# Pacing the background work of a decoder block: dearer choices, an idle background beside the query products, a gate table in four parts, and choices placed next to their gathers

## The chip, the cores and the metric

The kernel runs on one core of a Trainium2 chip. The metric is the device time of one execution in microseconds. Most executions of this kernel agree within 0.3%.

## The reference

One decoder block on 1024 tokens of width 1024, in float32. The second half of it is what the change is about:

```python
def peer_ffn(h, w_query, sub_keys, expert_u, expert_v):
    q = jnp.einsum('bsd,dk->bsk', h, w_query).reshape(B, S, 8, 2, 128)
    sc = jnp.einsum('bshpc,hpnc->bshpn', q, sub_keys)
    s1, i1 = lax.top_k(sc[..., 0, :], 16)
    s2, i2 = lax.top_k(sc[..., 1, :], 16)
    cand_s = (s1[..., :, None] + s2[..., None, :]).reshape(B, S, 8, 256)
    cand_i = (i1[..., :, None] * 128 + i2[..., None, :]).reshape(B, S, 8, 256)
    top_s, sel = lax.top_k(cand_s, 16)
    idx = jnp.take_along_axis(cand_i, sel, axis=-1)
    gates = jax.nn.softmax(top_s, axis=-1)
    ...
    u = expert_u[ec]
    a = jax.nn.gelu(jnp.einsum('cd,chkd->chk', xc, u), approximate=False) * wc
    return jnp.einsum('chk,chkd->cd', a, expert_v[ec])
```

The first half of the block is a normalisation, one wide input projection, a causal pooling mixer and a forgetting attention of 16 heads, an output projection and a residual addition. Each token then chooses 128 of 16384 experts (8 heads, 16 each), and an expert is one row of `expert_u` and one of `expert_v`.

## The kernel before

**Phases.** The tokens go through the first half in three phases of 512, 256 and 256 tokens, numbered 0, 1 and 2 (`phase`). A phase does attention with its input projections (`w_in`), then the output projection (`w_out`), then the query products (`w_query`, 16 chunks), each chunk followed on DVE by the top 16 of the scores. Matrix products in float32 are done as three products of high and low halves (`mm3`), and the halves of a weight are made by ScalarE (high) and DVE or POOL (low). Phases 0, 1 and 2 hold token tiles 0 to 3, 4 and 5, 6 and 7, of 128 tokens each.

**Two ways of computing the experts.** Tiles 1 to 5 (640 tokens) are computed densely: all 16384 experts are multiplied through, in 16 groups. A group is eight calls of `up` (a weight of 512 KB, 48 products, Gelu, times the gate table, split into halves `ah`, `al`) and eight of `down` (a weight, 48 products, added into `accT`). The gate table of a group, `Gg`, 2560 KB, is read back from DRAM, where `gates` wrote it. `finish_dense` transposes, normalises and stores. Tiles 0, 6 and 7 are computed by `experts`: 128 gathers of rows of `peer_u` by an indirect DMA issued on POOL (L900), each with a dot product on DVE (L915), then 128 of `peer_v`, each accumulated on DVE (L925), then the end of the tile (L929 to L939). The gathers are kept in program order on POOL; five row buffers are in turn.

**Background work.** `choose(tt)` turns the scores of a tile into 128 expert numbers and gates, nearly all on DVE (L858 is its most frequent line, 32 instructions per choice). `gates(gb, tt)` turns a chosen dense tile into its part of the gate table with DVE, POOL, TensorE (L983, 32 units) and ScalarE, and writes it to DRAM. `choose`, `gates` and `experts` are generators: each `yield` gives the cost at which the piece of work before the next one is booked. The work in front (`proj`, the attention units, `up`, `down`) calls `tick(us)` with a planner's time of what it has just issued; `tick` adds that time times `bg["rate"]` to a credit, and background pieces are issued while the credit is positive:

```python
        bg["credit"] += us * bg["rate"]
        while bg["todo"] and bg["credit"] > 0:
            cost = next(bg["todo"][0], None)
            ...
                bg["credit"] -= cost
```

`drain` issues all that is left without asking for credit. `RATES` holds the rates: the first for phase 1, the second for the attention of phase 2, the fourth for its output projection and queries, the third for the dense stage. The list in phase 1 is choice 0, choice 1, gates 1, choice 2, gates 2, choice 3, gates 3; phase 2 adds choice 4, gates 4, choice 5, and behind its attention gates 5. What is left is drained before the dense stage. There the list is choices 6 and 7, then the gathers of tiles 0, 6 and 7.

What the generators fix is the order of the program. A scheduler then sets the order on each engine: an instruction that is ready may go ahead of earlier ones that are not, except those that are kept in program order.

Of the kernel before, what the change touches and what calls it, by code (L numbers as in the profile page):

```python
# [37 lines left out]
XJ = 5  # L38
HP = 500
WX = (0, 0, 0)  # L40
RATES = (0.75, 0.6, 0.68, 0.7)
WL = ((0, 1), (0, 1), (0, 1))
C_U, C_Q, C_K, C_V, C_F, C_GA, C_GB = 0, 4, 12, 20, 28, 29, 37

# [2 lines left out]
def block_kernel(ctx: ExitStack, tc: tile.TileContext, I, out, dbg=None):  # L47
# [433 lines left out]
    def phase(c, nxt):  # L481
# [294 lines left out]

        tv = [sel.tile([128, PH, 2, 16], F, name="mv", tag="mv", bufs=4) for _ in range(NQ)]
        tx = [sel.tile([128, PH, 2, 16], U32, name="mxi", tag="mxi", bufs=4) for _ in range(NQ)]
        for ch in range(16):
            h, half = ch // 2, ch % 2  # L780
            z = proj(c, ("w_query", ch), h2h, h2l) if ch else z0
            if p == 2 and ch % 2:
                for x in range(2):
                    tc.keep_in_program_order(mv(W["h2"][x][:, ch // 2], h2dT[x][:, ch // 2]))
            q2 = c.tile("full", 3)
            nc.scalar.activation(q2, z, AF.Copy)
            ky = big.tile([128, 128], F, name="ky", tag="ky", bufs=2)
            nc.sync.dma_start(ky, I["keys"][ch])
            ps = pt_tile()[:, :n]
            for i in range(NQ):  # L790
                nc.tensor.matmul(ps[:, i * 128:(i + 1) * 128], q2[:, i * 128:(i + 1) * 128], ky,
                                 start=True, stop=True)
            sc = big.tile([128, n], F, name="sc", tag="sc", bufs=1)
            nc.scalar.activation(sc, ps, AF.Copy)
            for i in range(NQ):
                s_ = sc[:, i * 128:(i + 1) * 128]
                m_, x_ = tv[i][:, h, half], tx[i][:, h, half]
                tmp = sel.tile([128, 128], F, name="tmp", tag="tmp", bufs=2)
                nc.vector.max(m_[:, 0:8], s_)
                nc.vector.max_index(x_[:, 0:8], m_[:, 0:8], s_)  # L800
                nc.vector.match_replace(tmp, m_[:, 0:8], s_, -3e38)
                nc.vector.max(m_[:, 8:16], tmp)
                nc.vector.max_index(x_[:, 8:16], m_[:, 8:16], tmp)
        store_parts()
        big.release()
        return nc_, [choose(qb0 + i, tv[i], tx[i]) for i in range(NQ)]

    def choose(tt, mv_, mx_):
# [8 lines left out]
        for o, r0, r1, w in ((0, 0, 2, 16), (32, 2, 4, 8), (48, 4, 16, 4)):  # L817
# [1 line left out]
            full = [128, PH, r1 - r0, w]  # L819
            nc.vector.tensor_tensor(dst, a1[:, :, r0:r1, None].to_broadcast(full),  # L820
                                    b1[:, :, None, 0:w].to_broadcast(full), op=OP.add)
        yield 3.0
        ts = sel.tile([128, PH, 16], F, name="ts", tag="ts", bufs=1)
        ti = sel.tile([128, PH, 16], U32, name="ti", tag="ti", bufs=1)
        for h in range(PH):
            tmp = sel.tile([128, 128], F, name="tmp", tag="tmp", bufs=2)[:, :96]
            nc.vector.max(ts[:, h, 0:8], cand[:, h])
            nc.vector.max_index(ti[:, h, 0:8], ts[:, h, 0:8], cand[:, h])
            nc.vector.match_replace(tmp, ts[:, h, 0:8], cand[:, h], -3e38)
            nc.vector.max(ts[:, h, 8:16], tmp)  # L830
            nc.vector.max_index(ti[:, h, 8:16], ts[:, h, 8:16], tmp)
            if h % 2:
                yield 1.8
        tif = ti.rearrange("p h k -> p (h k)")
        ra, rb, w0, w1, pf = (pk[:, i * 128:i * 128 + 128] for i in range(5))
        u0 = sel.tile([128, 128], U32, name="u0", tag="u0", bufs=1)
# [16 lines left out]
        for half, r, dst in ((0, ra, w0), (1, rb, w1)):  # L853
            r4 = r.rearrange("p (h k) -> p h k", k=16)
            for part, to in ((0, dst), (1, pf)):
                for x in range(8):
                    v = mxf[:, :, half, part * 8 + x:part * 8 + x + 1].to_broadcast([128, PH, 16])
                    nc.vector.scalar_tensor_tensor(oh[:, :, :, x], r4, float(part * 8 + x), v,  # L858
                                                   op0=OP.is_equal, op1=OP.mult)
                    if x % 4 == 3:  # L860
                        yield 0.8
                nc.vector.tensor_reduce(to, oh.rearrange("p h k x -> p (h k) x"), axis=AX.X, op=OP.add)
                yield 1.1
            nc.vector.tensor_add(dst, dst, pf)
        gt = sel.tile([128, PH, 16], F, name="gate", tag="gated" if dense else f"gate{tt}", bufs=1)
        nc.vector.tensor_tensor(gt, ts, ts[:, :, 0:1].to_broadcast([128, PH, 16]), op=OP.subtract)
# [133 lines left out]
    def dense_experts():  # L1000
        h2h, h2l = W["h2"]
        wcount[1] = (0, 1)
        dd = tpool("dd", "right")
        W["x"], W["m"], W["i"] = dd, 1, 2
        X["p"] = dd
        acc = dd.tile([128, 8, ND], F, name="accT")
        A = {}

        def up(e):
            if e % 8 == 0:  # L1010
                A["G"] = dd.tile([128, NC16, 8, 16], F, name="Gg", tag="Gg", bufs=1)
                nc.sync.dma_start(A["G"], Gd[e // 8].rearrange("p c (i t) -> p c i t", i=8))
            wh, wl = load_w(I["ut"][e])
            G = A["G"][:, :, e % 8, :]
            A[e] = []
            for h in range(2):
                z = d_tile("z")[:, :NH]
                T = slice(h * NH, h * NH + NH)
                for k in range(8):
                    mm3(z, wh[:, k], wl[:, k], h2h[:, k, T], h2l[:, k, T], k == 0, k == 7)  # L1020
                ah = dd.tile([128, NH], R, name="ah", tag="ah", bufs=16)
                al = dd.tile([128, NH], R, name="al", tag="al", bufs=16)

                nc.scalar.activation(z, z, AF.Gelu)
                z3 = z.rearrange("p (c t) -> p c t", t=16)
                nc.vector.tensor_tensor(z3, z3, G[:, h * NC16 // 2:(h + 1) * NC16 // 2], op=OP.mult)
                split(ah, al, z, nc.vector)
                A[e].append((ah, al))
                tick(12 * ND * 0.00043)

        def down(gr, c):
            wh, wl = load_w(I["vt"][gr * 8 + c], nc.gpsimd)
            for h in range(2):
                o = d_tile("oT")[:, :NH]
                T = slice(h * NH, h * NH + NH)
                for i in range(8):
                    ah, al = A[gr * 8 + i][h]
                    mm3(o, wh[:, i], wl[:, i], ah, al, i == 0, i == 7)
                if gr == 0:
                    nc.vector.tensor_copy(acc[:, c, T], o)  # L1040
                else:
                    nc.vector.tensor_tensor(acc[:, c, T], acc[:, c, T], o, op=OP.add)
                if gr == 15:
                    nc.vector.scalar_tensor_tensor(acc[:, c, T], acc[:, c, T], gt2[:, c:c + 1], A["x1"][:, c, T],
                                                   op0=OP.mult, op1=OP.add)
            tick(24 * ND * 0.00043)

        def finish_dense(i, rows, fg):
            ps = [f() for f in ((pt_tile, pt_tile), (z_tile, z_tile), (s_tile, s_tile))[i % 3]]
            ss = cst.tile([128, 4], F, name="ss", tag="ssd", bufs=2)  # L1050
            yt = rows[:, i * D:i * D + D]
            hs = (slice(0, 512), slice(512, 1024))
            for hf, (pt, H) in enumerate(zip(ps, hs)):
                for c in range(4):
                    nc.tensor.transpose(pt[:, c * 128:(c + 1) * 128],
                                        acc[:, hf * 4 + c, i * 128:(i + 1) * 128], ident)
                nc.scalar.activation(yt[:, H], pt, AF.Square, accum_out=ss[:, hf:hf + 1])
            rs = rstd(ss)
            for pt, H in zip(ps, hs):
                nc.vector.scalar_tensor_tensor(yt[:, H], pt, rs, fg[:, H], op0=OP.mult, op1=OP.mult)  # L1060
            nc.sync.dma_start(out[(DT0 + i) * 128:(DT0 + i + 1) * 128, :], yt)

        for gr in range(16):
            for i in range(8):
                up(gr * 8 + i)
            if gr == 15:

                A["x1"] = W["hx"].tile([128, 8, ND], F, name="h2x0", tag="h2x0")
                fg = W["hx"].tile([128, ND // 128, D], F, name="h2x1", tag="h2x1")
                nc.sync.dma_start(A["x1"], x1dT)  # L1070
                nc.sync.dma_start(fg[:, 0], I["final_g"].partition_broadcast(128))
                rows = A["G"].rearrange("p a b c -> p (a b c)")
            for i in range(8):
                down(gr, i)
        for i in range(DT1 - DT0):
            finish_dense(i, rows, fg[:, 0])
        W["m"], X["p"] = 0, None
        drain()
        dd.release()
# [40 lines left out]
    bank["free"] = False  # L1120
    psx.release()
    X["ps"] = tc.alloc_tile_pool(name="psg", bufs=1, space=PS, reuse_waits="tile")
    bg["todo"] = ch + late + [experts(tt) for tt in range(DT1, 8)]
    bg["rate"] = RATES[2]
    dense_experts()
    X["ps"].release()
# [57 lines left out]
```

## Time and profile before

| | |
|---|---|
| median of three runs | 3362.7 us (3359.74 to 3367.93) |
| profiled execution, its own time | 3367.48 us |
| its span, first to last instruction | 3365.7 us |
| TensorE products, busy | 3132.3 us (93%), mean granted clock 0.968 |
| DVE, ScalarE, POOL busy | 2427.5, 1267.7, 1754.1 us |
| transfers | 1004.60 MB, mean 298 GB/s |

Busy shares are averages over stages with different limits: the dense stage, from about 1492 us on, and the phases before it are to be read one by one, by windows. TensorE's busy time is modelled from pipelined products; where it is full, the count of products in a window says more.

### The profile page before, as it was taken

How to read it: one execution, taken by the hardware profiler on the slowest of the kernel's cores; microseconds unless marked ns; L12 is line 12 of the kernel's file. 1: busy time of each engine (PE TensorE's matmuls, PEld its weight loads, DVE VectorE, ACT ScalarE, POOL GpSimd, SP SyncE). 2: the span in 40 equal slices, each digit the busy share in tenths (PEclk: the TensorE clock that was granted, in tenths of full speed). 3: DMA queues.
4: the chain of work that ended last, by engine and by line, in shares of the span. 5: the costliest groups of instructions: out<-in, count | busy, mean ns of one | idle time of the engine just before them, and what ended most of it. 6: DMA issues, size and time to landing. Idle time of an engine off the chain costs nothing. (4 is left out here: it accounts for less than half of the span.)

```text
span 3365.7 us, 56878 instructions
## 1 busy us (share of the span) xinstructions
PE 3132.3 (93%) x20912; PEld 2992.4 (89%) x20912; DVE 2427.5 (72%) x5520; ACT 1267.7 (38%) x2405; POOL 1754.1 (52%) x1328
## 2 busy tenths in 40 slices
PE   6999889888799899888999999999999999999995
PEld 4778778778788798888999999999999999999994
DVE  5764556997958876768766777677677767777677
ACT  5555542346545565522222322232223222322231
POOL 1233233013324132414777787678777767777774
PEclk9999999899999999999999999999999999999997
DMA  8987787777789788783899899899998999989997
GB/s 330 332 299 261 271 297 270 240 231 235 226 304 313 226 268 269 259 311 139 306 333 332 320 328 337 318 348 332 339 329 321 322 330 344 346 319 337 329 337 252
DMA packets 373078, 1004.60 MB, mean 298 GB/s; under 512 B 34128, under 2 KB 146368, under 8 KB 370624
## 3 DMA queue, kind: packets, MB, share of 16 engines
q1 hardware_dynamic: 262208, 598.26, 51.7%
q0 software_dynamic: 110592, 402.70, 32.7%
q8 instruction: 166, 2.72, 0.3%
q14 instruction: 112, 0.92, 0.1%
HBM read 851.25 MB, written 149.58 MB: 297 GB/s over the span
## 5 line engine op out<-in xcount | busy, mean ns | idle before, releaser
L233 POOL TENSOR_TENSOR wl<-wr,wh 128x1024 fp32r<-128x1024 f32 x320 | 776.1, 2426 | 647.7 <-ACT wh L232 604.4
L232 ACT ACTIVATE wh<-wr 128x1024 fp32r<-128x1024 f32 x325 | 344.2, 1059 | 927.5 <-PE oT L280 536.1
L279 PE MATMUL oT<-ah,wh 128*128 128x320 f32 x2048 | 632.3, 310 | 10.0 <-ACT ah L232 10.0
L279 PE MATMUL z<-h2x,wh 128*128 128x320 f32 x2048 | 633.8, 310 | 3.3 <-ACT wh L232 1.7
L281 PE MATMUL z<-h2x,wl 128*128 128x320 f32 x2048 | 633.5, 310 | 1.4 <-POOL wl L233 1.3
L280 PE MATMUL oT<-al,wh 128*128 128x320 f32 x2048 | 633.0, 310 | 1.2 <-DVE al L233 1.1
L280 PE MATMUL z<-h2x,wh 128*128 128x320 f32 x2048 | 633.3, 309 | 0.0
L281 PE MATMUL oT<-ah,wl 128*128 128x320 f32 x2048 | 632.7, 310 | 0.0
L925 DVE SCALAR_TENSOR_TENSOR acc<-g,dots,acc 128x1024 f32<-128x1024 f32 x381 | 489.2, 1284 | 124.9 <-DMA g<-peer_v,idx 122.3
L915 DVE SCALAR_TENSOR_TENSOR g<-g,h 128x1024 f32<-128x1024 f32 x384 | 460.9, 1214 | 94.2 <-DMA g<-peer_u,idx 92.4
L900 POOL DMA_INDIRECT g<-peer_v,idx x384 | 362.0, 943 | 126.1 <-issue 45.7
L900 POOL DMA_INDIRECT g<-peer_u,idx x384 | 361.7, 942 | 124.1 <-issue 57.1
L279 PEld LDWEIGHTS oT<-ah,wh 128*128 128x128 f32 x2048 | 384.9, 188 | 10.5 <-ACT ah L232 10.5
L279 PEld LDWEIGHTS z<-h2x,wh 128*128 128x128 f32 x2048 | 385.0, 188 | 4.2 <-ACT wh L232 2.2
L281 PEld LDWEIGHTS z<-h2x,wl 128*128 128x128 f32 x2048 | 384.8, 188 | 2.4 <-POOL wl L233 2.4
L280 PEld LDWEIGHTS oT<-al,wh 128*128 128x128 f32 x2048 | 385.1, 188 | 1.8 <-DVE al L233 1.8
L281 PEld LDWEIGHTS oT<-ah,wl 128*128 128x128 f32 x2048 | 385.1, 188 | 0.0
L280 PEld LDWEIGHTS z<-h2x,wh 128*128 128x128 f32 x2048 | 384.9, 188 | 0.0
L971 POOL TENSOR_TENSOR o<-hi,lo 128x512 f32<-128x512 f32 x160 | 206.6, 1293 | 322.2 <-PE G L983 283.0
L279 PE MATMUL z<-hTh,wh 128*128 128x256 f32 (+1 forms) x840 | 290.0, 350 | 18.2 <-ACT hTh L232 8.4
L281 PE MATMUL z<-hTh,wl 128*128 128x256 f32 (+1 forms) x840 | 286.3, 341 | 1.0 <-DMA wl<-w_inl 0.8
L280 PE MATMUL z<-hTl,wh 128*128 128x256 f32 (+1 forms) x840 | 285.9, 340 | 1.3 <-DVE hTl L233 1.3
(286 smaller groups left out, 5938.0 us busy)
## 6 DMA issues: line engine op xcount, KB each, us to landing
wr<-ut SPq DMA_DIRECT2D x128, 512.0 KB
wr<-vt SPq DMA_DIRECT2D x128, 512.0 KB
Gd<-Gb SPq DMA_DIRECT2D x40, 1024.0 KB
Gg<-Gd SPq DMA_DIRECT2D x16, 2560.0 KB
wh<-w_inh SPq DMA_DIRECT2D x60, 512.0 KB
wl<-w_inl SPq DMA_DIRECT2D x60, 512.0 KB
wm<-w_mod SPq DMA_DIRECT2D x48, 512.0 KB
wr<-w_in SPq DMA_DIRECT2D x45, 512.0 KB
```

Source lines behind the costliest of these rows:

```text
L232: nc.scalar.activation(hi, src, AF.Copy)
L233: eng_lo.tensor_tensor(lo, src, hi.bitcast(F), op=OP.subtract)
L279: nc.tensor.matmul(ps, ah, bh, start=start, stop=False)
L280: nc.tensor.matmul(ps, ah, bl, start=False, stop=False)
L281: nc.tensor.matmul(ps, al, bh, start=False, stop=stop)
L900: d = nc.gpsimd.indirect_dma_start(out=g, out_offset=None, in_=table, in_offset=bass.IndirectOffsetOnAxis(ap=col, axis=0))
L915: nc.vector.scalar_tensor_tensor(g, g, 1.0, h2, op0=OP.mult, op1=OP.mult, accum_out=dots[:, k:k + 1])
L925: nc.vector.scalar_tensor_tensor(acc, g, dots[:, k:k + 1], acc, op0=OP.mult, op1=OP.add)
L971: nc.gpsimd.tensor_tensor(o2, hi[:, X, :, None].to_broadcast([128, 4, 8, 16]), lo[:, X, None, :].to_broadcast([128, 4, 8, 16]), op=OP.mult)
```

## The change

A choice is booked at 34.3 instead of 24.0 (each `yield` but its last times about 1.5). The rates go from 0.75, 0.6, 0.68, 0.7 to 0.92, 0.95, 0.74, 0.95. Beside the 16 chunks of query products of every phase the rate is 0, so that no background piece is issued there. The gate table of a group is loaded in four parts of 10 of its 40 token chunks, 640 KB each, behind the second, fourth, sixth and eighth weight of the `down` calls of the group before; the first group's four parts stand ahead of the first `up`. In the dense stage the list becomes the gathers of tile 0, choice 6, the gathers of tile 6, choice 7, the gathers of tile 7.

```diff
-RATES = (0.75, 0.6, 0.68, 0.7)
+RATES = (0.92, 0.95, 0.74, 0.95)
...
+        rate, bg["rate"] = bg["rate"], 0.0
         for ch in range(16):
...
         store_parts()
+        bg["rate"] = rate
         big.release()
...
-        yield 3.0
+        yield 4.5
...
-                yield 1.8
+                yield 2.7
...
-                        yield 0.8
+                        yield 1.2
...
-                yield 1.1
+                yield 1.6
...
+        def load_gates(gr, part):
+
+            if part == 0:
+                A["G"] = dd.tile([128, NC16, 8, 16], F, name="Gg", tag="Gg", bufs=1)
+            C = slice(part * NC16 // 4, (part + 1) * NC16 // 4)
+            nc.sync.dma_start(A["G"][:, C], Gd[gr][:, C].rearrange("p c (i t) -> p c i t", i=8))
+
         def up(e):
-            if e % 8 == 0:
-                A["G"] = dd.tile([128, NC16, 8, 16], F, name="Gg", tag="Gg", bufs=1)
-                nc.sync.dma_start(A["G"], Gd[e // 8].rearrange("p c (i t) -> p c i t", i=8))
...
             wh, wl = load_w(I["vt"][gr * 8 + c], nc.gpsimd)
+            if gr < 15 and c % 2:
+                load_gates(gr + 1, c // 2)
...
+        for part in range(4):
+            load_gates(0, part)
         for gr in range(16):
...
-    bg["todo"] = ch + late + [experts(tt) for tt in range(DT1, 8)]
+    bg["todo"] = late + [f for i, tt in enumerate(range(DT1, 8)) for f in (ch[i], experts(tt))]
```

## Rows read from the trace of the kernel before

**Rows 1.** Windows by stage; columns as in the head line.

```profile
core 0: us, PE busy (x) PEld busy (x) DVE busy (x) ACT busy (x) POOL busy (x), PEclk, DMA share, GB/s
...
596.00:933.00 337.00, 280.58 (x2067) 267.46 (x2066) 296.83 (x979) 177.76 (x407) 83.28 (x76) 0.90 0.72 232
...
982.00:1051.00 69.00, 65.98 (x537) 64.73 (x538) 53.34 (x265) 24.53 (x45) 22.55 (x21) 0.98 0.91 313
1051.00:1379.00 328.00, 296.18 (x2295) 278.48 (x2294) 261.01 (x703) 194.47 (x416) 98.36 (x94) 0.96 0.80 253
...
1492.00:1600.00 108.00, 92.14 (x581) 89.01 (x582) 97.94 (x341) 34.05 (x55) 43.45 (x24) 0.92 0.43 155
1600.00:3321.00 1721.00, 1720.13 (x11733) 1719.82 (x11732) 1238.48 (x1881) 459.09 (x746) 1288.83 (x990) 1.00 0.91 329
```

**Rows 2.** Windows of 60 us in the dense stage, columns as in rows 1.

```profile
2200.00:2260.00 60.00, 60.00 (x412) 60.00 (x411) 48.01 (x93) 20.25 (x39) 51.45 (x41) 1.00 0.98 357
...
2800.00:2860.00 60.00, 60.00 (x412) 60.00 (x411) 42.39 (x80) 12.68 (x19) 47.12 (x36) 1.00 0.97 358
```

**Rows 3.** Windows of 20 us at the dense start, columns as in rows 1.

```profile
1540.00:1560.00 20.00, 17.36 (x112) 16.31 (x112) 19.09 (x97) 7.89 (x14) 4.79 (x2) 1.00 0.24 80
1560.00:1580.00 20.00, 9.10 (x38) 8.27 (x39) 18.98 (x52) 6.03 (x12) 4.96 (x2) 0.66 0.28 97
```

**Rows 4.** Windows, the instructions of L858 alone (32 per choice).

```profile
690.00:757.00 67.00, 10.19 (x32) 0.95 0.76 246
757.00:933.00 176.00, 10.80 (x32) 0.90 0.72 226
...
1492.00:1600.00 108.00, 24.02 (x64) 0.92 0.43 155
```

**Rows 5.** The gathers' line L900, duration, first and last start.

```profile
L900 POOL DMA_INDIRECT g<-peer_u,idx x384: 932/938/1134, 1583.2 to 3048.2; - x192
```

**Rows 6.** Timeline of TensorE, its last weight product.

```profile
3317.59 0.31 PE L281 MATMUL oT<-ah,wl 128*128 128x320 f32 x1
```

**Rows 7.** Timeline of all engines behind the last weight product.

```profile
3319.53 0.60 PE L1055 MATMUL s<-ident,accT 128*128 128x128 f32 x4
...
3321.00 1.28 ACT L223 ACT_TABLE_LOAD   x1
3321.29 0.48 DVE L1042 TENSOR_TENSOR accT<-accT,oT 128x320 f32<-128x320 f32 x1
...
3322.88 0.54 DVE L1044 SCALAR_TENSOR_TENSOR accT<-accT,modc,h2x 128x320 f32<-128x320 f32 x1
...
3331.57 0.59 ACT L1057 ACTIVATE Gg<-pt 128x512 f32<-128x512 f32 x1
...
3338.28 1.40 DVE L1060 SCALAR_TENSOR_TENSOR Gg<-pt,ss,h2x 128x512 f32<-128x512 f32 x2
...
3340.97 0.29 ACT L223 ACTIVATE ss<-ss,epsc 128x1 f32<-128x1 f32 x1 [1.23 <-DVE ss L222]
...
3355.23 1.29 DVE L925 SCALAR_TENSOR_TENSOR acc<-g,dots,acc 128x1024 f32<-128x1024 f32 x1 [1.07 <-DMA g<-peer_v,idx]
...
3362.08 0.34 SPq L939 DMA_DIRECT2D out<-r  x1
```

**Rows 8.** Groups of DVE's instructions by line, 1600 to 3321.

```profile
L925 DVE SCALAR_TENSOR_TENSOR acc<-g,dots,acc 128x1024 f32<-128x1024 f32 x368 | 472.4, 1284 | 114.6 <-DMA g<-peer_v,idx 112.0
L915 DVE SCALAR_TENSOR_TENSOR g<-g,h 128x1024 f32<-128x1024 f32 x378 | 453.7, 1214 | 89.5 <-DMA g<-peer_u,idx 87.7 <-DVE accT L1042 0.3
```

**Rows 9.** Groups of POOL's instructions by line, 1600 to 3321.

```profile
L233 POOL TENSOR_TENSOR wl<-wr,wh 128x1024 fp32r<-128x1024 f32 x242 | 584.9, 2417 | 203.7 <-ACT wh L232 196.7 <-PE oT L281 5.2
L900 POOL DMA_INDIRECT g<-peer_u,idx x375 | 353.0, 941 | 121.8 <-issue 55.5 <-DVE g L915 25.0 <-DVE al L233 7.5
```

**Rows 10.** Windows, the gate products of L983 alone (TensorE and its weight loads).

```profile
982.00:1051.00 69.00, 13.73 (x104) 12.77 (x104) 0.98 0.91 313
1051.00:1379.00 328.00, 74.33 (x536) 68.07 (x536) 0.96 0.80 253
```

**Rows 11.** Waits of ScalarE, 1600 to 3300: total us, times, longest.

```profile
ACT wh L232 <- DMA wr<-vt: 134.3, 17, 12.2
```

## Prediction

> **What bounds the kernel now.** I read the windows by stage first [rows 1]: the two attention phases with background work (596 to 933 and 1051 to 1379 us), the query products of the first of them (982 to 1051), the start of the dense stage (1492 to 1600) and its long rest (1600 to 3321). In the rest TensorE is busy 1720.13 of 1721 us at full clock: no wait is left there, and only less matrix work could shorten it. Time can be won in three places: before the dense stage (TensorE idles 56 us of the first attention phase and 32 of the second, at granted clocks of 0.90 and 0.96), at its start, and behind its last product.
>
> Shorter windows show the start. A steady stretch holds 412 products per 60 us [rows 2], 137 per 20; 1540 to 1560 holds 112 and 1560 to 1580 only 38, behind whose idle part the granted clock averages 0.66, between its levels of 1.2 and 2.4 GHz [rows 3]. The 124 missing products are 18 us. DVE is full in both: the choices of token tiles 6 and 7 run there, 64 of the 256 instructions of L858 [rows 4], and the first gather of an expert row is issued at 1583.2 [rows 5].
>
> Last the end, in order of time [rows 6, 7]. The last weight product ends at 3317.9, the span at 3365.7: 47.8 us in which TensorE has only transposes left. What runs is gathers, each waiting for its transfer, and the end of tile 7 behind them: its last accumulation starts at 3355.23, its output is issued at 3362.08. So the program's end is set by background work that did not fit beside the dense stage.
>
> **The change, part by part.** First the pace of the dense stage, from the kernel's own booking. An `up` ticks 2 x 12 x 640 x 0.00043 = 6.605, a `down` the same; 256 of them give 1690.8. Old: 1690.8 x 0.68 = 1149.7 credits against two choices at 24.0 and three `experts` at 257 x 1.46 = 375.2, together 1173.7. It is 24.0 short, 16 gathers at 1.46 each, and those are the tail. New: 1690.8 x 0.74 = 1251.2 against 2 x 34.3 + 1125.7 = 1194.3. The background ends at 95.5% of the stage, some 80 us before its last product. The gathers stand in a fixed place among the weight splits on POOL, so they cannot lag far behind the products that they were booked beside.
>
> Behind the last product there is then only `finish_dense`, for the token tiles that need it: an addition and a scaling (0.48 + 0.54), transposes (0.6), two squares of 0.59 for each of three tiles (3.5), a square root with its neighbours (0.7), one table load (1.3), two products on DVE (1.4), and from issuing the output to the end of the span 3365.7 - 3362.1 = 3.6 [rows 7]. That is 11.6; with the hand-overs I take 13. The squares of all five tiles in a row would make it 16. The tail goes from 47.8 to 13: **-35 us** (32 to 36).
>
> Second, the choices put next to their tiles. Tile 0's gathers start at once, the choice of tile 6 comes a tile later. DVE is busy 97.94 of 108 us at the start [rows 1]; its own dense share elsewhere is (1238.48 - 472.4 - 453.7) / 1721 = 18% [rows 1, 8], 20 us, so the two choices cost 35 to 40 us of DVE each. If they run late in the stage, beside dense work alone (no gather is booked during a choice), DVE has room, and the 18 us of products lost at the start come back. But place in the program is not place in time: in the trace, choices ran ahead of their place. The third, booked behind the first gate tile, has all its 32 instructions of L858 at 690 to 757, and the fourth, booked behind the second, runs before 933 [rows 4]. If the new ones come forward too, they fill the gaps that gathers leave on DVE. At the new pace a unit of 7.04 us holds 6.605 x 0.74 / 1.46 = 3.35 gathers: on DVE 3.35 x 1.28 + 18% x 7.04 = 5.6 us, 79%; on POOL 3.35 x 0.94 + 2.42 = 5.6 us, 79% [rows 8, 9]. Two choices, up to 80 us, then fill DVE for 80 / 0.21 = 380 us, and products wait for DVE as they do now, spread out. Between 0 and the whole 18 I take half: **-9 us** (+10 to -18).
>
> Third, the bookings before the dense stage. By the end of attention in the first of the two phases the old credit is 180 x 0.75 = 135, which buys choices 0 and 1, gates 1, choice 2, gates 2 (24.0 and 32 each, 136); the new is 180 x 0.92 = 166, for the same at 34.3 and 32 (167). The content is the same; a choice is a little thinner, a gate tile a little denser. Since the choices run ahead of their booking anyway, I put this at 0, with 10 us either way from the 56 us of idle there.
>
> Fourth, nothing beside the query products. Gate products take 13.73 us of TensorE in the query of that phase, which is busy 65.98 of 69 us there [rows 1, 10]; they move into the second attention phase, where it idles 32 us. The new rate there, 0.95 for 205 ticks, gives 195 credits against 8 + 32 + 34.3 + 32 + 34.3 = 141, so it fits. Behind it gates 5 has 20 credits in the output projection, and 12 of its 32 are left to `drain`, at the dense start. Between winning those 13 us and paying as much elsewhere (DVE is busy 261 of 328 us there already) I take **-4 us** (+12 to -13).
>
> Fifth, the gate table in four parts: 640 KB after every second `down` weight instead of 2560 KB at once. Today weights come late in places: ScalarE waits 134.3 us in 17 waits for those of `down`, the longest 12.2 [rows 11], and TensorE still never waits in that stage [rows 1]. The weights held ahead cover it, so 0. The Trainium skill, "DMA: Bandwidth & Descriptors", section "Measured (HBM→SBUF, 128 partitions, SWDGE, issued from GpSimd)", speaks against the split: it asks for transfers of at least 1 MiB. By the fixed cost of some 2 us that its section "Anatomy of one DMA" gives, four parts would take an estimated 6 us more than one whole, and fifteen tables 90 us if that lay on the path; no run here shows it.
>
> **The sum.** The profiled execution took 3367.5 us beside its span of 3365.7. 3367.5 - 35 - 9 - 4 = 3319.5. It lay 4.8 above the median of the three runs, so against that I forecast 3315.
>
> **The rivals.**
> *The choices come forward and fill DVE.* Then the start gains nothing or loses 10: 3324 to 3334. For it: the choices ahead of their place. Against: gathers and dense work come first in program order now, so a choice only gets what they leave.
> *The denser background hurts attention.* Gates 3 in the second phase instead of beside the query, gates 5 drained late: +12 instead of -4, 3331. For it: TensorE idles there while DVE is busy 88% and 80%. Against: those 32 us of idle can take gate products.
> *The other side: transfers become the bound.* A unit moves 3.35 x 0.524 MB of gathers, 0.524 of weights and 0.164 of gate table, 2.44 MB in 7.04 us: 347 GB/s, against 329 at the old pace [rows 1]. If the ceiling were C, the 1521 ticks of gathers, 1621 us, stretch by 347/C - 1. That takes back all 48 us at C = 337; at 329 it costs 89 and ends near 3404. Against it: stretches of 60 us at 357 and 358 GB/s with TensorE at 60.00 of 60 [rows 2]. For it: the DMA share there is already 0.98 and 0.97.
> *The split table delays weights.* The mean wait is 134.3 / 17 = 7.9 us. Were it doubled, 15.8 would exceed by 3.6 the 12.2 that is covered today; fifteen times that is 54 us, 3369, no gain. Against: the parts hold the same bytes and lie between weights. (It is what the Trainium skill objects on "DMA: Bandwidth & Descriptors", put in this kernel's rows.)
> *It does nothing to the end.* Were the gathers 80 us late, the tail would stay: 3350.
>
> **Chances.** Forecast 0.55 (3302 to 3326), choices on DVE 0.20, attention hurt 0.12, transfers 0.06, split table 0.04, no effect on the end 0.03. The first three end faster by over 0.3%, 10 us, about what a measurement of this kernel can tell from no change; the last, the upper end of the third and the lower ends of the two transfer cases lie about within it. Faster 0.87, same 0.06, slower 0.07. The range 3296 to 3342 takes in the first three cases with the bounds of their terms and leaves out the rest.
>
> **What the profile after should show.** No gather behind the last weight product, and a span end 12 to 16 us behind it. A first gather before 1510 instead of 1583. No count under 120 products per 20 us at the start; L858 late in the dense stage if the choices keep their place, in its first 400 us if not. No gate product beside the query products. DMA near 347 GB/s in the long stretch with TensorE still full; waits of TensorE there, for weight halves of POOL or ScalarE, would prove the transfers or the split a bound and the prediction wrong.

## The result, and the profile after

| | before | after |
|---|---|---|
| median of the runs | 3362.39 us (3359.74 to 3367.93, four runs) | 3332.12 us (3331.02 to 3334.94, four runs) |
| profiled execution, its span | 3367.48, 3365.7 us | 3331.02, 3329.3 us |
| first dense product to the end of the last | 1493.9 to 3317.9 | 1489.9 to 3311.8 |
| behind the last dense product | 47.8 us | 17.5 us |

After divided by before is 0.9909, 95% interval 0.9892 to 0.9926: faster by 0.9%, some 30 us, where 48 were forecast (the kernel before has one run more here than in the table ahead of the prediction). The 36.4 us between the two spans divide into 4.0 ahead of the dense stage, 2.1 in it (1824.0 to 1821.9) and 30.3 behind it. Nearly all of the gain is the tail.

First the windows by stage, cut where this kernel's stages begin and end, to be held against [rows 1].

```profile
core 0: us, PE busy (x) PEld busy (x) DVE busy (x) ACT busy (x) POOL busy (x), PEclk, DMA share, GB/s
589.00:926.00 337.00, 281.44 (x2076) 266.92 (x2075) 300.91 (x980) 177.25 (x409) 84.98 (x77) 0.91 0.73 232
978.00:1039.00 61.00, 54.23 (x425) 53.33 (x426) 31.91 (x213) 11.27 (x30) 0.34 (x2) 0.94 0.85 305
1039.00:1373.00 334.00, 299.96 (x2375) 282.49 (x2373) 282.53 (x751) 204.00 (x426) 110.80 (x106) 0.98 0.81 253
1488.00:1700.00 212.00, 199.87 (x1313) 196.77 (x1312) 201.41 (x554) 61.86 (x105) 143.25 (x107) 0.97 0.84 295
1700.00:3311.00 1611.00, 1611.00 (x10986) 1611.00 (x10985) 1164.62 (x1716) 433.86 (x694) 1200.51 (x918) 1.00 0.91 328
3311.00:3329.00 18.00, 6.50 (x46) 5.15 (x44) 9.34 (x22) 7.36 (x25) 0.00 (x0) 0.69 0.37 147
```

The queries of phase 1 take 61 us instead of 69, with POOL all but idle: the background is gone from them. The attention behind them takes 334 instead of 328. The long dense stretch is full at full clock as before. The last window has no POOL instruction: no gather stands behind the last product.

The gathers' line, duration and first and last start, against [rows 5]:

```profile
L902 POOL DMA_INDIRECT g<-peer_u,idx x384: 932/938/1764, 1492.4 to 2967.2; - x192
L902 POOL DMA_INDIRECT g<-peer_v,idx x384: 932/938/955, 1802.6 to 3246.7; - x192
```

They begin 91 us earlier and end 65 us ahead of the last product. Next the dense start in windows of 20 us, against [rows 3], and the most frequent line of the choices in two stretches, against [rows 4]:

```profile
1520.00:1540.00 20.00, 16.96 (x97) 16.71 (x98) 19.96 (x48) 9.96 (x17) 16.02 (x12) 0.83 0.84 288
1540.00:1560.00 20.00, 19.29 (x131) 19.03 (x131) 20.00 (x44) 6.66 (x13) 13.57 (x11) 1.00 0.75 260
1640.00:1660.00 20.00, 14.19 (x85) 13.40 (x84) 20.00 (x41) 5.74 (x12) 12.66 (x11) 0.89 0.84 287
...
1488.00:1590.00 102.00, 11.98 (x32) 0.97 0.81 293
1590.00:1700.00 110.00, 14.29 (x32) 0.97 0.87 296
```

Both choices, booked one tile of gathers and two tiles behind the start, ran in the first 200 us (1497 to 1586 and 1584 to 1686). DVE is full beside them, and two windows hold 97 and 85 products where a steady one holds 137. The holes have moved and are fewer, but the products lost are nearly the same. (Lost time here and below is the sum over the dense stage of what the gap between two successive product starts has above the steady 0.1465 us, gaps over 0.16 us counted: 21.6 us before, 19.6 after.)

Last the tail, in order of time, against [rows 7]:

```profile
3311.48 0.31 PE L281 MATMUL oT<-ah,wl 128*128 128x320 f32 x1
3311.63 1.04 PE L1063 MATMUL pt<-ident,accT 128*128 128x128 f32 x8
...
3312.26 0.60 ACT L1065 ACTIVATE Gg<-pt 128x512 f32<-128x512 f32 x1 [20.59 <-PE pt L1063]
...
3316.59 9.41 SPq L1069 DMA_DIRECT2D out<-Gg  x5
...
3321.73 0.58 ACT L1065 ACTIVATE Gg<-z 128x512 f32<-128x512 f32 x1
...
3324.23 1.41 DVE L1068 SCALAR_TENSOR_TENSOR Gg<-z,ss,h2x 128x512 f32<-128x512 f32 x2
```

The tail is `finish_dense` alone. The squares of the five dense tiles run on ScalarE from 3312.26 to 3322.31, the products on DVE that scale the tiles follow from 3315.15 to 3325.64, and 3.7 us behind them the last output has landed.

### The profile page after: what moved, and what is told of

Read it like the earlier page. It is cut to its first block, busy times and chain, and to the rows that moved or that the text cites. A ratio compares the mean times of both kernels' runs of the same rounds, so it can differ in the third digit from the quotient of the medians.

```text
span 3329.3 us, 56918 instructions
## 1 busy us (share of the span) xinstructions
PE 3123.0 (94%) x20912; PEld 2982.7 (90%) x20912; DVE 2440.7 (73%) x5520; ACT 1266.9 (38%) x2405; POOL 1754.0 (53%) x1328
## 4 chain that ended last, share of the span: by engine, by line
PE 59%; DVE 11%; DMA 3%; ACT 1%; issue 1%; POOL 0%; SPq 0%; DVEq 0%; ACTq 0%; POOLq 0%
PE z L281 10%; PE z L279 10%; PE z L280 10%; PE oT L280 8%; PE oT L279 8%; PE oT L281 8%; PE G L985 3%; DVE g L917 2%; DVE cand L860 1%; DVE o L975 1%; DMA wl<-w_queryl 1%; DVE pk L864 1%; DMA wr<-w_queryl 1%; DVE mx L585 1%; ACT Gb L986 1%
## 5 line engine op out<-in xcount | busy, mean ns | idle before, releaser
L973 POOL TENSOR_TENSOR o<-hi,lo 128x512 f32<-128x512 f32 x160 | 199.9, 1252 | 300.0 <-PE G L985 245.4
L1050 DVE TENSOR_TENSOR accT<-accT,oT 128x320 f32<-128x320 f32 x240 | 116.5, 487 | 233.6 <-PE oT L281 232.8
```

What stands on the lines that cost most here:

```text
L973: nc.gpsimd.tensor_tensor(o2, hi[:, X, :, None].to_broadcast([128, 4, 8, 16]), lo[:, X, None, :].to_broadcast([128, 4, 8, 16]), op=OP.mult)
```

## The experiments

Each kernel is compared with the kernel before on its own chip; a kernel with one run has no interval.

**The tail: the rate alone, the rate left out, the list alone.** The first is the kernel before with one number changed.

```diff
-RATES = (0.75, 0.6, 0.68, 0.7)
+RATES = (0.75, 0.6, 0.74, 0.7)
```

> The kernel before with the dense stage's rate alone raised from 0.68 to 0.74. Theory of the tail: 1251.2 credits cover the 1173.7 that the old booking asks for, so no gather is left behind the last weight product, the tail goes from 48 to about 17.5 us as in the changed kernel, and everything ahead of it stays: about 3362 - 31 = 3331 us, the whole gain of the change. Rival, that the new list order is needed (gathers from 1492 instead of 1583): the tail stays at 40 us or more, 3355 or above.

Measured: 3337.03 us (3335.07 to 3340.01, four runs), ratio 0.9916 (0.9892 to 0.994). The long stretch and the end:

```profile
1600.00:3318.00 1718.00, 1718.00 (x11716) 1717.99 (x11716) 1255.14 (x1898) 464.68 (x741) 1300.97 (x1001) 1.00 0.92 334
3318.00:3335.00 17.00, 5.27 (x41) 4.08 (x39) 10.12 (x23) 7.36 (x25) 0.00 (x0) 0.81 0.47 187
```

The tail is 17.5 us, as after the whole change, and POOL has nothing in it. One number gives a ratio that the interval of the whole change doesn't tell from it. Its margin was thin: here the last gather starts at 3302.6, 15 us ahead of the last product at 3318.0.

The second is the kernel after with the dense rate put back.

```diff
-RATES = (0.92, 0.95, 0.74, 0.95)
+RATES = (0.92, 0.95, 0.68, 0.95)
```

> The changed kernel with the dense stage's rate put back from 0.74 to 0.68. Theory of the tail: 1149.7 credits against 1194.3 leave 44.6, some 30 gathers, behind the last weight product instead of the 16 of before; at the 2.2 us per gather of the old tail that is a tail of about 75 to 85 us and 3390 to 3400 us in all, later than before the change. Rival, that the list order brings the gain: 3335 or less.

Measured: 3391.81 us (one run; before on that chip 3367.24). The last product starts at 3306.53, the last gather at 3372.3, the span ends at 3390.1. Two windows behind the last product:

```profile
3320.00:3340.00 20.00, 0.52 (x3) 0.12 (x1) 12.86 (x19) 2.21 (x9) 6.56 (x7) 0.50 0.87 297
3340.00:3360.00 20.00, 0.00 (x0) 0.00 (x0) 11.93 (x10) 0.00 (x0) 8.43 (x9) 0.50 0.79 240
```

TensorE has next to nothing, and POOL runs 16 instructions, the gathers that are left, in 40 us. The tail is 83.2 us, longer than the 47.8 before, because the choices are booked dearer: 1149.7 credits against 1194.3 are 44.6 short, 31 gathers. The trace has 27 behind the last product, issued from 3307.6 to 3372.3, one per 2.5 us, and the end of the tile takes the other 17.8 us. (In the kernel before there are 12 where the credits give 16, from 3318.9 to 3349.5, with 16.2 us behind them.) So the arithmetic of credits sets the tail, in both directions, though it is four gathers too high both times, and the dearer booking of the choices lengthens the tail unless the rate is raised.

The third is the kernel before with the new list.

```diff
-    bg["todo"] = ch + late + [experts(tt) for tt in range(DT1, 8)]
+    bg["todo"] = late + [f for i, tt in enumerate(range(DT1, 8)) for f in (ch[i], experts(tt))]
```

> The kernel before with the list order of the dense stage alone changed (tile 0's gathers, choice 6, tile 6, choice 7, tile 7), its rates and bookings as before. Theory of the tail: 24.0 credits stay uncovered, the 16 gathers stay behind the last product, and the choices come forward to the dense start as they do in the changed kernel: 3358 to 3364 us. Rival, that the order gives back the lost start: 3342 to 3350.

Measured: 3367.62 us (3357.86 to 3380.9, ten runs), ratio 1.0011 (0.9994 to 1.0029): nothing. The tail is 46.4 us, the lost products 25.1. The dense start:

```profile
1490.00:1600.00 110.00, 100.00 (x647) 97.89 (x648) 107.92 (x331) 32.03 (x53) 72.02 (x52) 0.97 0.79 286
```

It holds 66 products more than the kernel before has in a window two microseconds shorter [rows 1], but DVE is fuller, and the choices run at 1494 to 1577 and 1573 to 1664 beside gathers. The loss is spread, not gone.

**The choices: held late, and woven in.** Can the lost products be had back? First the kernel after, with the three additions that begin a late choice held at their place in the program.

```diff
+            d = nc.vector.tensor_tensor(dst, a1[:, :, r0:r1, None].to_broadcast(full),
...
+            if tt >= DT1:
+                tc.keep_in_program_order(d)
```

> The changed kernel with the first additions of choices 6 and 7 kept in program order on DVE, so that each choice runs behind its predecessor tile's gathers, where the list puts it, and not ahead of them. If the products lost at the dense start (about 20 us of TensorE between 1490 and 1690) are due to the choices coming forward, they come back: 3312 to 3320 us. Rival, that the start is lost to something else or that a choice costs as much later in the stage: 3328 to 3336.

Measured: 3337.0 us (3330.35 to 3338.86, five runs), ratio 0.9909 (0.9887 to 0.993), no better than the kernel after. The choices did go where the list has them, to 2096 and 2717 us. The first of them:

```profile
2100.00:2120.00 20.00, 20.00 (x139) 20.00 (x138) 19.22 (x84) 10.09 (x17) 6.09 (x3) 1.00 0.25 80
2120.00:2140.00 20.00, 16.14 (x98) 15.61 (x98) 17.35 (x40) 3.98 (x7) 6.50 (x5) 0.91 0.35 118
```

The choice fills DVE, POOL has 3 and 5 instructions per 20 us and the transfers fall to 80 GB/s: the gathers stop, for 58 us, since the next tile's need the choice. Where it ends products are lost there too, 98 of 137 in the second window. In all 16.6 us are still lost in the dense stage: 6.2 at the start, where no choice runs any more, 5.9 at the end of the first choice, and 4.5 near 2800 us, some 50 us behind the second, with the gathers going again. And since the gathers stood still twice, the last starts at 3310.3 and the tail is 20.3. The step "if they run late, DVE has room, and the 18 us come back" fell: as one block a choice costs about as much late as early.

So a choice has to be thin, not late. In the next kernel each late choice is issued in pieces, one behind every eighth gather of the tile before, with its DVE instructions held in program order (`Kept`, not shown, hands each of them to `tc.keep_in_program_order`).

```diff
+    def weave(long, short, every):
+        n = 0
+        for cost in long:
+            yield cost
+            n += 1
+            if n % every == 0:
+                more = next(short, None)
+                if more is not None:
+                    yield more
+        yield from short
...
+        vec = Kept() if tt >= DT1 else nc.vector
...
-    bg["todo"] = late + [f for i, tt in enumerate(range(DT1, 8)) for f in (ch[i], experts(tt))]
+    bg["todo"] = [weave(late[0], ch[0], 8), weave(experts(DT1), ch[1], 8), experts(DT1 + 1)]
```

> The changed kernel with the choices of tiles 6 and 7 woven in pieces into the gathers of the tile before (a piece behind every eighth gather) and every DVE instruction of theirs kept in program order. The run with kept choices lost 6 us at the dense start, 6 and 4.5 at its two choices, and stopped the gathers for 58 us at each. If what a choice costs is DVE filled for 40 us in one piece, the pieces fit (79% of DVE in gathers and dense work, 7% more) and the losses at the choices go, without the stops: the dense stage loses 6 to 9 us of products instead of 20, the tail stays at 17.5, 3316 to 3324 us. Rival, that any DVE work of a choice costs products: 3328 or more.

Measured: 3323.01 us (3321.19 to 3323.92, four runs), ratio 0.9868 (0.9845 to 0.9892). Start and end:

```profile
1490.00:1700.00 210.00, 204.75 (x1375) 203.45 (x1374) 164.56 (x420) 59.66 (x101) 150.40 (x112) 0.98 0.88 318
3304.00:3322.00 18.00, 5.79 (x44) 4.60 (x42) 9.33 (x22) 7.35 (x25) 0.00 (x0) 0.82 0.37 147
```

DVE is busy 165 of 210 us at the start instead of 201 of 212, and 62 more products fit in two microseconds less. The dense stage takes 1811.2 us with 8.8 lost, the tail is 17.5 again. None of its runs is as slow as the fastest of the kernel after (on another chip, where the kernel before has a median of 3367.43). To see whether the other parts add to this, the same weave was put on the kernel before, with the dense rate 0.74 and nothing else of the change.

```diff
-RATES = (0.75, 0.6, 0.68, 0.7)
+RATES = (0.75, 0.6, 0.74, 0.7)
...
-    bg["todo"] = ch + late + [experts(tt) for tt in range(DT1, 8)]
+    bg["todo"] = [weave(late[0], ch[0], 8), weave(experts(DT1), ch[1], 8), experts(DT1 + 1)]
```

> The kernel before with two edits alone: the dense stage's rate at 0.74, and the choices of tiles 6 and 7 woven into the gathers of the tile before and kept in order on DVE; old bookings, old query rate, gate table in one load. Theory, that the tail and the choices are all there is: as the woven kernel, a tail of 17.5 us and 5 to 9 us of products lost in the dense stage, 3318 to 3328 us, a ratio of 0.985 to 0.989. Rival, that the dearer choices, the empty queries or the four parts carry some of the gain: 3330 or more.

Measured: 3322.05 us (3320.87 to 3326.64, four runs), ratio 0.9874 (0.9856 to 0.9893).

```profile
1486.00:1700.00 214.00, 209.97 (x1424) 208.50 (x1424) 167.74 (x401) 60.74 (x100) 161.99 (x122) 1.00 0.92 332
3299.00:3318.00 19.00, 6.93 (x45) 6.36 (x44) 9.33 (x22) 8.65 (x26) 0.00 (x0) 0.75 0.35 139
```

Lost in the dense stage 9.3 us, tail 19.2: the same time without dearer choices, without the idle background beside the queries and without the split table. Every run of both kernels lies below every run of the one after, though the intervals of the ratios just touch its interval; nothing else of the change is needed for it.

Part of the loss at the start may not be the choices'. In the kernel after 6.2 of its 19.6 us lie between 1520 and 1540 us; the woven kernel loses 6.8 there without a choice in one block, and the one with late choices 4.5 without any. That window, first of the woven kernel, then of the kernel before with rate and weave:

```profile
1520.00:1540.00 20.00, 16.40 (x92) 15.87 (x91) 16.17 (x32) 8.23 (x15) 15.85 (x13) 0.83 0.78 266
1520.00:1540.00 20.00, 20.00 (x139) 20.00 (x138) 16.14 (x32) 8.31 (x16) 17.03 (x13) 1.00 0.96 339
```

In the woven kernel POOL stands still for 4.9 and 5.1 us before two gathers (issued at 1515.2 and 1521.3), until DVE is done with their row buffers, and the weight split behind them comes late. The eight kernels with the gathers first and the table in four parts hold 92 to 129 products in this window, the two with the gathers first and the table in one load 135 and 139. No run here changes the table's first load alone, so its part in this is not shown.

**The pace of the gathers: a higher rate, more row buffers.** The kernel after books 540 us per tile of 256 gathers (375.2 credits at 4.888 per unit of 7.04 us), but its tiles took 594.9, 571.5 and 564.9 us. What holds them?

```diff
-RATES = (0.92, 0.95, 0.74, 0.95)
+RATES = (0.92, 0.95, 0.8, 0.95)
```

> The changed kernel with the dense stage's rate at 0.80 instead of 0.74: 1352.6 credits against 1194.3, gathers booked at 500 us a tile. In the changed kernel a tile took 565 to 572 us where 540 were booked. If that is the gathers' own pace (a row buffer's round of transfer, DVE and POOL), a tile stays at 555 to 572 us, TensorE loses nothing and the time is 3326 to 3337. Rival, that transfers at 367 GB/s are asked for and hold back the weights too: TensorE waits in the long stretch and the time is 3350 or more.

Measured: 3340.9 us (one run; before there 3367.43); tiles of 599.9, 570.8 and 568.7 us. The time is 4 us above the theory's upper end: against the kernel after the dense stage begins 5.1 us later and loses 4.6 us more, at its start. Though 8% more credit is given, the pace is the same. POOL's groups of 2700 to 3220 us, first of the kernel after, then of this one:

```profile
L233 POOL TENSOR_TENSOR wl<-wr,wh 128x1024 fp32r<-128x1024 f32 x75 | 181.6, 2421 | 47.8 <-ACT wh L232 46.7
L902 POOL DMA_INDIRECT g<-peer_u,idx x121 | 113.9, 942 | 38.6 <-issue 19.1 <-DVE g L917 13.1 <-DVE accT L1050 3.0
L902 POOL DMA_INDIRECT g<-peer_v,idx x115 | 108.2, 941 | 33.0 <-issue 14.6 <-DVE acc L927 7.7 <-DVE al L233 3.8
```

```profile
L233 POOL TENSOR_TENSOR wl<-wr,wh 128x1024 fp32r<-128x1024 f32 x75 | 181.6, 2421 | 52.6 <-ACT wh L232 44.4 <-issue 7.3
L902 POOL DMA_INDIRECT g<-peer_u,idx x124 | 116.7, 941 | 36.9 <-issue 21.3 <-DVE g L917 10.0 <-DVE al L233 1.8
L902 POOL DMA_INDIRECT g<-peer_v,idx x109 | 102.6, 941 | 30.5 <-issue 20.6 <-DVE acc L927 4.4 <-DVE al L233 1.5
```

There are 236 gathers for 75 weight splits in the one and 233 for 75 in the other, 3.1 per split, where the booking has 3.35 and 3.62. Counted over the whole stage, the last gather of either kernel stands behind split 249 of 256, and the ends of the half tiles behind the same splits (43, 84, 127, 167, 209). So the order on POOL came with the program and not from the times of a run: the scheduler lets weight splits go ahead of gathers that were booked before them. POOL still waits some 45 us for ScalarE's halves in these 520, so it isn't full either. Which of its reasons the scheduler goes by stays open. A third row buffer beside the two that were added in the dense stage tests one of them:

```diff
-GMORE = 2
+GMORE = 3
```

> The changed kernel with six row buffers for the gathers instead of five. If a buffer's round sets the gathers' pace, a tile's 256 gathers take about the booked 540 us instead of 565 to 572, and the last gather is issued near 3200 instead of 3247; the time stays, since the end is the dense stage's: 3326 to 3336. Rival, that the transfers themselves are at their limit (DMA share 0.93): 560 to 570 us a tile still.

Measured: 3335.27 us (one run); tiles of 591.0, 568.9 and 557.7 us.

```profile
2700.00:3220.00 520.00, 520.00 (x3548) 520.00 (x3547) 376.53 (x576) 133.36 (x211) 400.49 (x311) 1.00 0.93 339
```

POOL has 311 instructions here as in the kernel after (236 + 75): the buffers don't set the pace. In all three kernels TensorE is full, at 337 to 339 GB/s, so the rival of the transfers shows in none; but the 347 GB/s of the forecast were not reached, and what the transfers would do there stays untried.

**The gate table alone.** The kernel before with the loads in four parts, by the `load_gates` of the change.

```diff
...
             wh, wl = load_w(I["vt"][gr * 8 + c], nc.gpsimd)
+            if gr < 15 and c % 2:
+                load_gates(gr + 1, c // 2)
...
+        for part in range(4):
+            load_gates(0, part)
```

> The kernel before with the gate table loaded in four parts behind the second, fourth, sixth and eighth weight of a group's down calls, and nothing else. Theory, that the loads are covered by the weights held ahead: no difference, 3358 to 3368 us, a ratio within 0.3% of 1, TensorE without a wait between 1600 and 3300. Rival, that the fixed costs of four loads delay the weights: slower by 10 us or more.

Measured: 3367.99 us (3358.49 to 3375.16, ten runs), ratio 1.0007 (0.9994 to 1.0021). ScalarE's wait for the `down` weights, against [rows 11], and the only wait of TensorE from 1600 to 3300 us:

```profile
ACT wh L232 <- DMA wr<-vt: 191.3, 28, 15.8
...
PE oT L280 <- DVE al L233: 0.7, 1, 0.7
```

The parts do delay weights: 191.3 us in 28 waits instead of 134.3 in 17, the longest 15.8 instead of 12.2. In the kernel after they are 207.6, 31 and 15.0; over all profiles the four kernels with one load have 119 to 134 us, the nine with parts 156 to 236. But the weights held ahead cover that too, and TensorE's one wait of 0.7 us is not for a weight. The Trainium skill, "DMA: Bandwidth & Descriptors", section "Measured (HBM→SBUF, 128 partitions, SWDGE, issued from GpSimd)", asks for at least 1 MiB per transfer, measured there on loads issued from GpSimd. These loads are issued on SyncE, and the parts of 640 KB cost nothing that reaches the end here.

**Ahead of the dense stage: queries, and the booking.** First the kernel after without the idle background beside the queries.

```diff
-        rate, bg["rate"] = bg["rate"], 0.0
...
-        bg["rate"] = rate
```

> The changed kernel without the zero rate beside the query products. The query products of phase 1 took 61 us in the changed kernel against 69 before, and the attention behind them 334 against 328. Theory, that the gate products only move: the queries go back to 67 to 69 us, the attention behind to 328 to 332, and the time stays within 3 us, 3329 to 3336. Rival, that the empty queries are a gain of their own: 3338 to 3341.

Measured: 3344.89 us (3341.41 to 3346.89, four runs), ratio 0.9933 (0.9909 to 0.9958). That is above both forecasts as they stand; by the ratio it would be 3340 us on the chip of the kernel after, within the rival's 3338 to 3341. But its interval overlaps that of the kernel after. The query of phase 1 and the attention behind it:

```profile
985.00:1053.00 68.00, 61.83 (x499) 60.62 (x500) 46.80 (x250) 19.74 (x41) 16.89 (x16) 0.97 0.81 285
1053.00:1388.00 335.00, 299.65 (x2365) 280.88 (x2364) 277.93 (x725) 204.44 (x424) 104.08 (x103) 0.98 0.81 255
```

The query takes 68 us instead of 61, and the attention is no shorter for it. Yet from the end of phase 0's queries to the first dense product (the former read to a whole microsecond) it is 901.6 us, against 900.9 in the kernel after; the rest of the difference is a later end of phase 0 and 6.3 us more of lost products at the dense start. Whether this part is worth anything isn't settled.

Then the kernel after with the choices booked as before.

```diff
-        yield 4.5
+        yield 3.0
...
-                yield 2.7
+                yield 1.8
...
-                        yield 1.2
+                        yield 0.8
...
-                yield 1.6
+                yield 1.1
```

> The changed kernel with the choices booked as before (24.0 instead of 34.3 credits), all else changed. Theory, that the choices run as early as DVE lets them whatever they are booked at: no difference to the changed kernel, 3328 to 3340 us, the eight choices and five gate tiles within 10 us of their places in it up to the dense stage. Rival, that the dearer booking spares the attention phases: the first attention phase longer than 345 us instead of 337, 3345 or more.

Measured: 3353.62 us (3349.12 to 3362.93, nine runs), ratio 0.9971 (0.9958 to 0.9985), slower than the kernel after by 21 us. The rival's time came, but not at its place: the first attention phase took 339 us, not over 345. The first attention phase, the queries of phase 1 and the attention behind them, and then the gate products alone (TensorE and its weight loads) beside the output projection and beside those queries:

```profile
593.00:932.00 339.00, 285.82 (x2145) 272.36 (x2144) 309.16 (x997) 186.05 (x418) 89.76 (x87) 0.92 0.75 237
988.00:1062.00 74.00, 69.15 (x568) 68.15 (x568) 45.00 (x225) 29.91 (x48) 24.81 (x21) 0.98 0.95 307
1062.00:1403.00 341.00, 295.87 (x2243) 275.78 (x2241) 267.70 (x730) 189.35 (x409) 87.81 (x85) 0.95 0.76 240
...
932.00:988.00 56.00, 15.12 (x108) 14.11 (x109) 0.94 0.93 313
988.00:1062.00 74.00, 22.09 (x158) 19.84 (x157) 0.98 0.95 307
```

With cheaper choices the new rates issue gate tiles earlier, and their products run beside the output projection and, though the rate is 0 there, beside the queries, which stretch to 74 us; the attention behind them takes 341. To the first dense product it is 912.8 us. The kernels with the new rates and the new booking need 896.6 to 903.2 (six of them, mean 900.4), those with the old of both 897.1 to 903.0 (five, mean 900.4). So dearer booking and higher rates belong together: the pair is worth nothing, the rates without the booking cost some 12 us. (Of the 19.0 us between the two spans, 4 more lie ahead of all that, in phase 0, and 3 in the dense stage.)

## Why the prediction was right or wrong, step by step

**The tail, forecast -35.** Right in mechanism, too large by 4.7: 47.8 to 17.5 us is -30.3, outside the 32 to 36 that it allowed. The mis-sized term is the 13 us of `finish_dense` (its parts add up to 12.1, not to the 11.6 given). It counted the scaling on DVE for one tile, 1.4 us; after, those of all five tiles are on the chain that ends last, 5 x 1.41 = 7 us. The transposes of the fourth tile wait until the first is scaled:

```profile
3315.15 1.41 DVE L1068 SCALAR_TENSOR_TENSOR Gg<-pt,ss,h2x 128x512 f32<-128x512 f32 x2
3315.96 1.32 PE L1063 MATMUL pt<-ident,accT 128*128 128x128 f32 x8 [1.55 <-DVE Gg L1068]
```

Those of the fifth wait for the second in the same way, and the table load of 1.3 us that was counted does not occur behind the last product. The 16 us named as the bound, for five tiles' squares in a row, came near by luck: the squares stop twice to wait. That the credits set the tail is shown both ways by the rate alone and the rate left out.

**"The gathers stand in a fixed place among the weight splits on POOL, so they cannot lag far."** The place is fixed, but it isn't the booked one. The scheduler put 3.1 gathers to a split where 3.35 were booked, and as many where 3.62 were. So the last gather came 65 us ahead of the last product instead of 80, which cost nothing; in the kernel with the rate alone the margin was down to 15. The forecast of 347 GB/s fell with it (328 over the long stretch).

**The choices next to their tiles, forecast -9.** Wrong: the dense stage gained 2.1 us, its lost products went from 21.6 to 19.6. The rival that the choices come forward and fill DVE came true in its place, the first 200 us; the 3324 to 3334 that it gave took in the 3332 measured. The step itself failed twice over. Place in the list wasn't place in time, and where the place was forced the choice cost as much there, since a block of 35 to 40 us of DVE holds up the dense stage's own DVE work wherever it lies. Only cut in pieces did it give back 11 us.

**Bookings 0, queries -4.** The bookings are 0 as a pair, but not because the choices run ahead of them anyway: with the old booking the new rates cost 12 us. Of the queries, the 8 us that they win in the window are paid back by 6 in the attention behind, so much of the rival that the denser background hurts attention came true; its 12 us on balance did not. The pair of profiles has the dense stage starting 4.0 us earlier, as forecast, but for another reason: phase 0's queries, beside which no background stood before either, end 7 us earlier, and from there to the dense start it takes 3 us longer. Over eleven kernels the means are equal.

**The gate table, 0.** Right. Its rival had the mechanism, later weights, but not the price: the longest wait grew from 12.2 to 15.8 us and still reached no product.

**The sum.** Against the profiled execution 3319.5 was forecast and 3331.0 measured: 4.7 from the tail and 6.9 from the dense stage make the 11.5, but for the rounding. The range held the median of 3332; the 3302 to 3326 of the forecast itself did not. The signs that the text named for right and wrong were read as they came: no gather behind the last product, a first gather at 1492.4, no gate product beside the queries

```profile
978.00:1039.00 61.00, 0.00 (x0) 0.00 (x0) 0.94 0.85 305
1039.00:1373.00 334.00, 81.63 (x608) 74.13 (x608) 0.98 0.81 253
```

(TensorE and its weight loads, gate products alone, against [rows 10]), no wait of TensorE in the long stretch; but a span end 17.5 us behind the last product instead of 12 to 16, and windows of 97 and 85 products instead of none under 120.

**Left open.** Why the scheduler lets splits go ahead of gathers, what the 6 us between 1520 and 1540 are due to, whether the idle background beside the queries is worth its few microseconds, and what 347 GB/s would do.

## What to carry to other kernels

Work out what a background list costs against the credit that it gets before looking at anything finer: the shortfall, times the pace of that work when it runs alone, with the end of its last item behind it, is about the tail, and one number can remove it. A block of background work that filled an engine for tens of microseconds cost the foreground about the same early or late here; cut it into pieces behind instructions that are kept in order, and read from the trace where they went. When several parts of a change come together, run each alone, or leave it out: here one of five carried the gain, and two were neutral only as a pair.

## What the runs showed of the hardware that was not expected

A gather of 128 rows keeps POOL for 0.94 us, and the next one in a row starts 0.30 us behind its end. The forecast's 79% for POOL left that out. A stretch of the kernel after:

```profile
2897.79 2.43 POOL L233 TENSOR_TENSOR wl<-wr,wh 128x1024 fp32r<-128x1024 f32 x1
2900.38 0.95 POOL L902 DMA_INDIRECT g<-peer_u,idx  x1 [0.16 <-issue]
2901.64 0.94 POOL L902 DMA_INDIRECT g<-peer_u,idx  x1 [0.30 <-issue]
2902.88 0.94 POOL L902 DMA_INDIRECT g<-peer_u,idx  x1 [0.30 <-issue]
2904.55 2.41 POOL L233 TENSOR_TENSOR wl<-wr,wh 128x1024 fp32r<-128x1024 f32 x1 [0.73 <-ACT wh L232]
```

The first gather behind a split starts 0.16 us after it. With these a unit of one split and 3.35 gathers takes an estimated 2.42 + 0.16 + 3.35 x 0.94 + 2.35 x 0.30 = 6.4 of its 7.04 us on POOL, 91%, without any wait for another engine.
